# Three delta-rule preparations side by side, and attention's value products as three 16-bit products

## The chip, the cores and the metric

The kernel runs on one core of one Trainium2 chip. The metric is the device time of one execution in microseconds (us). The engines are TensorE (PE in the profile; its weight loads are PEld), VectorE (DVE), ScalarE (ACT), GpSimd (POOL) and SyncE (SP, which issues nearly all DMAs). Each engine works through its own instructions in the order in which they were put into its queue.

## The reference

Two layers of an encoder over 1024 tokens of width 1024, batch 1, float32. Each layer normalizes its input, projects it to 3448 columns, runs three groups of heads on them, multiplies by a SiLU gate, projects back and adds the residual. Cut to the two groups that the change touches:

```python
def gated_delta_chunked(q, k, v, g, beta):          # 6 heads of 64, two directions, 16 chunks of 64
    cum = jnp.cumsum(g, axis=-1)
    d_incl = jnp.exp(jnp.where(incl, cum[..., :, None] - cum[..., None, :], -jnp.inf))
    a_mat = beta[..., :, None] * jnp.einsum('nhcid,nhcjd->nhcij', k, k) * d_strict
    rhs = jnp.concatenate([beta[..., None] * v, (beta * gam)[..., None] * k], axis=-1)
    sol = lax.linalg.triangular_solve(a_mat, rhs, left_side=True, lower=True, unit_diagonal=True)
    ...
    def step(s, inp):                               # carries the 64x64 state from chunk to chunk
        u = u0_c - w_c @ s
        o = qg_c @ s + p_c @ u
        s = ge_c * s + kd_c.T @ u
        return s, o

def attend(q_blk):                                  # 6 heads, keys of 96 = 64 + 32 rotary, values of 64
    s = jnp.einsum('bqhd,bkhd->bhqk', q_blk, k)
    p = jax.nn.softmax(s, axis=-1)
    return jnp.einsum('bhqk,bkhd->bqhd', p, v)
```

The third group, RWKV-7, is scanned in chunks in the same way and is not changed.

## The kernel before

Each of the two layers (`layer`, L578) runs two streams of work at once. The **dense** stream (`dense_work`, L605) is a generator: the input projection (27 tiles of 128 columns, each as three 16-bit products, lines L371 to L373), then multi-head latent attention (`mla`, L1559). It yields, after each piece, a number of "units" that says how long the piece is held to be (0.65 for a group of three 512-column products). The **chain** stream is first the RWKV scan and then the delta rule (`gdn`, L1227). `chain` (L1155) runs in turns of a loop: in each turn it advances the scan `S` by one piece and each running preparation by one piece, and after each of these calls `tick`, which lets the dense stream advance by `dense / len(turn)` units. So the constant `DENSE_R` (RWKV) or `DENSE_G` (delta rule) is the number of dense units in one turn. What the turns record is then put in order on each engine by a scheduler; the TensorE orders of the two streams are tied to each other.

A **preparation** (`gdn_prep`, L1020) treats two chunks in both directions for two heads. It loads decays by DMA (`spread`, L1038), forms `gd_d`, `gd_pt`, `gd_g`, `gd_kb`, and then inverts a triangular matrix (`invert`, L897) in five doubling steps: a product into bank `pb` (L916), DVE's `z` (L942), its copy into a block-diagonal tile by ACT (L920) for one half and DVE (L921) for the other, then a product into `pb` and four into the bank `pe` (L959), evicted by ACT (L947, L960). There are 24 preparations per layer. `AHEAD_G = 2` lets two run at once, a new one starting when the last has made 10 pieces. Products into `pb` go to the bank of their parity (`B`, L304), of which 256 of 512 columns are used. A **step** of the scan (`gdn_step`, L1082) does one chunk: DVE makes `gs_r`, ACT `gs_u`, DVE the new state `gs_s`, with POOL's `gs_e` (L1104) as the decayed old state.

In **attention** the unit is a pair of heads and one half of the queries (`mla_main`, L1747): for each of 8 blocks of 128 keys and each head, three score products into one PSUM bank `pa` (L1765 to L1767), the exponential by ACT into a float32 tile `mp` (L1769), a running sum of these by POOL (L1771) for the denominator, and the product with the values in float32 (L1776). `pa` has three banks, one of which holds the unit's result. The rows' maxima come from products of their own (`mla_max`, L1732) that DVE reduces (L1733). `mla_v` (L1661) makes the values once per layer, in float32. `out_part` (L1855) does the part of the output projection that needs RWKV alone; it loads the residual by DMA into `mp` tiles and stores the sum.

## Time and profile before

| what | value |
|---|---|
| median of 3 runs | 2484.49 us (2482.22 to 2487.52) |
| the profiled execution | 2482.41 us, of which the span from the first to the last instruction is 2480.6 us |
| granted TensorE clock, mean | 0.952 |
| busy: PE, DVE, ACT, POOL | 91%, 66%, 56%, 35% of the span |
| layer 0, projection and RWKV | 0 to 585 us |
| layer 0, delta rule with attention | 585 to 1172 us |
| layer 0, output projection | 1172 to 1245 us |
| layer 1, the same three | 1245 to 1804, 1804 to 2395, 2395 to 2480.6 us |

The span is that of one profiled execution. A matmul's record is longer than the time it keeps PE from the next one, since matmuls are pipelined and their ends are modelled; the distance from one start to the next is what PE spends on it when nothing is late. In a row of groups, "x" is the count, then come the busy time and the mean of one in ns, and behind the bar the idle time before them with what ended it.

### The profile page before, as it was taken

How to read it: one execution, taken by the hardware profiler on the slowest of the kernel's cores; microseconds unless marked ns; L12 is line 12 of the kernel's file. 1: busy time of each engine (PE TensorE's matmuls, PEld its weight loads, DVE VectorE, ACT ScalarE, POOL GpSimd, SP SyncE). 2: the span in 40 equal slices, each digit the busy share in tenths (PEclk: the TensorE clock that was granted, in tenths of full speed). 3: DMA queues.
4: the chain of work that ended last, by engine and by line, in shares of the span. 5: the costliest groups of instructions: out<-in, count | busy, mean ns of one | idle time of the engine just before them, and what ended most of it. 6: DMA issues, size and time to landing. Idle time of an engine off the chain costs nothing.

```text
span 2480.6 us, 54956 instructions
## 1 busy us (share of the span) xinstructions
PE 2257.7 (91%) x21524; PEld 1384.0 (56%) x21524; DVE 1642.2 (66%) x3706; ACT 1384.2 (56%) x3077; POOL 865.8 (35%) x1095
## 2 busy tenths in 40 slices
PE   5999988999899999988989999899998999898988
PEld 4455655555576555554755565565556755555556
DVE  6557777755687766685345676877456777667755
ACT  5567556655555655555245765567464456455541
POOL 1133323323324544554012332342332256344430
PEclk9999999999899989999999999998998899899989
DMA  3121222213251111103212222222224311111041
GB/s 128 42 71 48 74 56 71 70 55 121 97 181 45 37 53 31 31 27 90 94 64 56 63 63 69 65 69 58 102 82 141 121 46 30 48 41 36 21 141 68
DMA packets 140338, 174.09 MB, mean 70 GB/s; under 512 B 37072, under 2 KB 95536, under 8 KB 140080
## 3 DMA queue, kind: packets, MB, share of 16 engines
q1 hardware_dynamic: 139936, 170.19, 22.8%
q8 instruction: 170, 2.79, 0.5%
q14 instruction: 88, 0.72, 0.1%
q0 software_dynamic: 144, 0.39, 0.1%
HBM read 106.88 MB, written 39.04 MB: 59 GB/s over the span
## 4 chain that ended last, share of the span: by engine, by line
PE 56%; DVE 20%; ACT 7%; issue 7%; POOL 5%; DMA 5%; SPq 0%; POOLq 0%; ACTq 0%; DVEq 0%
PE pa L371 5%; PE pa L372 5%; PE pa L373 5%; PE pa L1776 4%; PE pb L916 4%; DMA wf<-in_w_in_dram 3%; POOL wl L532 3%; PE pe L1339 2%; PE pa L1732 2%; DVE cacc L728 2%; PE pa L1765 2%; PE pe L833 2%; PE pe L959 2%; PE pc L1107 1%; PE pa L1767 1%
## 5 line engine op out<-in xcount | busy, mean ns | idle before, releaser
L373 PE MATMUL pa<-h,wl 128*128 128x512 f16 x864 | 332.4, 385 | 10.0 <-POOL wl L532 6.7
L371 PE MATMUL pa<-h,wh 128*128 128x512 f16 x864 | 333.7, 386 | 1.3 <-DVE h L484 1.3
L372 PE MATMUL pa<-h,wh 128*128 128x512 f16 x864 | 332.8, 385 | 0.0
L942 DVE TENSOR_TENSOR z<-pb,c 128x256 f16<-128x256 f32 (+1 forms) x320 | 155.3, 486 | 146.8 <-PE pb L916 141.1
L1771 POOL TENSOR_TENSOR md<-md,mp 128x512 f32<-128x512 f32 x144 | 192.2, 1337 | 149.5 <-ACT mp L1769 140.9
L920 ACT COPY bdz<-z 64x256 f16<-64x256 f16 (+1 forms) x384 | 173.4, 455 | 119.9 <-DVE z L942 95.1
L532 POOL TENSOR_TENSOR wl<-wf,wh 128x512 f16<-128x512 f32 x108 | 136.7, 1282 | 233.7 <-ACT wh L531 199.9
L947 ACT CAST x<-pb 128x256 f16<-128x256 f32 (+1 forms) x320 | 134.8, 421 | 106.1 <-PE pb L916 104.8
L960 ACT CAST xT<-pe 128x512 f16<-128x512 f32 x256 | 151.0, 590 | 55.6 <-PE pe L959 54.2
L1776 PE MATMUL pa<-mp,mv 128*64 128x512 f32 x384 | 177.0, 621 | 0.0
L1733 DVE TENSOR_REDUCE mmx<-pa 128x1 f32<-128x512 f32 x192 | 130.5, 685 | 34.4 <-PE pa L1732 32.0
L1404 POOL TENSOR_TENSOR rs_e<-rs_z,rw_em 64x128 f32<-64x128 f32 x120 | 55.7, 479 | 270.4 <-DVE rs_z L1431 242.0
L921 DVE COPY bdz<-z 64x256 f16<-64x256 f16 (+1 forms) x384 | 138.8, 365 | 13.1 <-PE pe L952 1.6
L1769 ACT ACTIVATE mp<-pa 128x512 f32<-128x512 f32 x192 | 114.6, 597 | 56.4 <-PE pa L1767 54.1
L916 PEld LDWEIGHTS <-bdgh 128*128 128x128 f16 x1920 | 92.1, 100 | 87.5 <-issue 52.8
L373 PEld LDWEIGHTS <-wl 128*128 128x128 f16 x864 | 85.5, 99 | 89.4 <-POOL wl L532 10.1
L916 PEld LDWEIGHTS <-xT 128*128 128x128 f16 x1600 | 77.3, 99 | 98.6 <-issue 64.9
L371 PEld LDWEIGHTS <-wh 128*128 128x128 f16 x864 | 90.0, 104 | 65.6 <-issue 10.8
L916 PE MATMUL pb<-z,xT 128*128 128x64 f16 x1600 | 108.6, 196 | 16.6 <-DVE z L942 15.6
L728 DVE SCALAR_TENSOR_TENSOR cacc<-raw,dv,cacc 128x512 f32<-128x512 f32 x144 | 120.8, 859 | 1.2 <-ACT cacc L722 0.7
L372 PEld LDWEIGHTS <-wh 128*128 128x128 f16 x864 | 85.5, 99 | 62.6 <-issue 8.2
L916 PE MATMUL pb<-x,bdgh 128*128 128x64 f16 x1600 | 106.1, 197 | 10.2 <-DVE x L937 7.2
(463 smaller groups left out, 5658.6 us busy)
## 6 DMA issues: line engine op xcount, KB each, us to landing
wf<-in_w_in_dram SPq DMA_DIRECT2D x54, 512.0 KB
q_d<-cacc SPq DMA_DIRECT2D x18, 512.0 KB
rw_ka<-rw_kr SPq DMA_DIRECT2D x32, 256.0 KB
rw_ka<-rw_ak SPq DMA_DIRECT2D x64, 128.0 KB
gate_d<-gate SPq DMA_DIRECT2D x16, 512.0 KB
wof<-in_w_out_dram SPq DMA_DIRECT2D x16, 512.0 KB
xp_d<-mp SPq DMA_DIRECT2D x32, 256.0 KB
xo<-xp_d SPq DMA_DIRECT2D x16, 512.0 KB
```

Of the source, the lines that this page charges most:

```text
L371: self.did = nc.tensor.matmul(out, lhsT=lh, rhs=rh, start=(first and idx == 0), stop=False)
L372: self.did = nc.tensor.matmul(out, lhsT=lh, rhs=rl, start=False, stop=False)
L373: self.did = nc.tensor.matmul(out, lhsT=ll, rhs=rh, start=False, stop=(last and idx == n - 1))
L532: nc.gpsimd.tensor_tensor(out=wl[:, ks], in0=wf[:, ks], in1=wh[:, ks], op=ALU.subtract)
L728: nc.vector.scalar_tensor_tensor(out=acc[:, c], in0=raw[:, c.start + k:c.stop + k], scalar=tap(k), in1=acc[:, c], op0=ALU.mult, op1=ALU.add)
L916: self.did = nc.tensor.matmul(ps[:, 64 * u:64 * u + 64], lhsT=st(lhsT, u), rhs=rhs(u), start=True, stop=True)
L920: nc.scalar.copy(zb[self.H[0], :, 0], t[self.H[0]])
L921: nc.vector.tensor_copy(zb[self.H[1], :, 1], t[self.H[1]])
L942: nc.vector.tensor_tensor(out=self.q8(z), in0=v(ps), in1=self.m8(self.c2(f"w{k}"), w), op=ALU.mult)
L960: nc.scalar.copy(xn[:, g:g + 4].rearrange("p u h i -> p (u h i)"), p2)
L1771: nc.gpsimd.tensor_tensor(out=acc[h], in0=prev[h] if t == 1 else acc[h], in1=pT, op=ALU.add)
L1776: self.did = nc.tensor.matmul(po[NR[h]], lhsT=vv[:, t, 2 * pr + h], rhs=pT[h], start=(t == 0), stop=(t == 7))
```

## The change

**Delta rule.** Three preparations run at once (`AHEAD_G` 3), a new one starting after 6 pieces of the last (the chain's argument 10 becomes 6). The block-diagonal tiles and the parities become three. The two banks `pb` are cut in halves of 256 columns, of which three are used (`halves`). `gd_g` no longer has a tile of its own but overwrites `gd_d`, behind `gd_pt`; `gs_r` and `gs_e` have one buffer instead of two; the result tile `X` is allocated at the end of the inversion. `DENSE_G` goes from 1.03 to 1.38 and `DENSE_R` from 1.0 to 0.95.

**Attention.** The values are scaled to the range of 16-bit floats (their scale is found with a reduction and a small product) and kept as a high and a low 16-bit part (ACT and DVE). The exponential is computed twice: in float32 and, as the high part, in 16 bits; the low part is their difference, by DVE for the first head and by POOL for the second. The product with the values is then high*high + low*high + high*low, with the two heads in turn. The first block's exponential is written straight into the running sum. The dense stream's number for the value products goes from 1.45 to 0.7 units. `mp` has 2 buffers instead of 5.

When the program is recorded it counts its turns and units. Before, a layer's RWKV scan takes 193 turns and its delta rule 279, with 246.3 of the 526.9 dense units done when RWKV ends. With the change it is 193 and 189 turns, and 236.55 of 490.9 units. In both the dense stream is exhausted when the delta rule ends.

```diff
-AHEAD_G = 2
+AHEAD_G = 3
...
-DENSE_R = 1.0
-DENSE_G = 1.03
+DENSE_R = 0.95
+DENSE_G = 1.38
...
     def B(self):
         if self.sx:
             return self.A()
+        if self.halves:
+            return self.halves[self.pty // 2][:, 256 * (self.pty % 2):256 * (self.pty % 2) + 256]
         return self.pb.tile([128, 512], F32, tag=f"b{self.pty}", name=self.nm("pb"))
...
+        self.ebias = self.cp.tile([128, 1], F32, name="ebias")
+        nc.vector.memset(self.ebias, math.log(16.0))
...
-        with self.phase("G", 6, "right"):
+        with self.phase("G", 5, "right"):
...
-        g = T("g", 1)
+        pt = T("pt", k)
+        nc.vector.tensor_tensor(out=fd(pt), in0=of(1), in1=fd(dd), op=ALU.mult)
+        g = dd
         nc.vector.tensor_tensor(out=fd(g), in0=of(0), in1=fd(dd), op=ALU.mult)
...
-        pt = T("pt", k)
-        nc.vector.tensor_tensor(out=fd(pt), in0=of(1), in1=fd(dd), op=ALU.mult)
...
-        X = T("x", k)
+        X = lambda: T("x", k - 1)
         yield
-        yield from self.invert(g, X)
+        X = yield from self.invert(g, X)
...
-            r = self.T("gs_r", [128, 2, 64], F32, 2)
+            r = self.T("gs_r", [128, 2, 64], F32, 1)
...
-                se = self.T("gs_e", [128, 2, 64], F32, 2)
+                se = self.T("gs_e", [128, 2, 64], F32, 1)
...
-                ps.append(thread(preparation, nxt, nxt % 2))
+                ps.append(thread(preparation, nxt, nxt % max(2, self.sets)))
...
     def gdn(self):
-        self.inv_tiles(2 * GW, 2)
-        self.chain([lambda hp=hp: self.gdn_open(hp) for hp in range(3)], 16 // GW, AHEAD_G, 0, 10, DENSE_G, self.gdn_prep, self.gdn_step, self.gdn_close)
+        self.inv_tiles(2 * GW, AHEAD_G)
+
+        self.halves = [self.pb.tile([128, 512], F32, tag=f"b{y}", name=self.nm("pb")) for y in range(2)]
+        self.chain([lambda hp=hp: self.gdn_open(hp) for hp in range(3)], 16 // GW, AHEAD_G, 0, 6, DENSE_G, self.gdn_prep, self.gdn_step, self.gdn_close)
+        self.halves = None
...
-        self.mv = self.T("mv", [128, 8, 6, 64], F32, 1)
+        c = self.U("mvs", [128, 5], F32, 2)
+        nc.vector.tensor_reduce(out=c[:, 0:1], in_=f, axis=AX.X, op=ALU.max, apply_absolute_value=True)
...
+        self.vs = c[:, 3:4]
+        self.mv = [self.T("mv" + x, [128, 8, 384], F16, 1) for x in "hl"]
...
-            nc.scalar.copy(self.mv[:, t].rearrange("p a v -> p (a v)"), ps[:, :384])
+            vh, vl = self.mv[0][:, t], self.mv[1][:, t]
+            nc.scalar.mul(vh, ps[:, :384], c[:, 4:5])
+            nc.vector.scalar_tensor_tensor(out=vl, in0=ps[:, :384], scalar=c[:, 4:5], in1=vh, op0=ALU.mult, op1=ALU.subtract)
...
-            pT = self.T("mp", [128, 512], F32, 5)
-            nc.scalar.activation(pT, ps, AF.Exp)
+            pT = self.T("mp", [128, 512], F32, 2) if t else acc[h]
+            nc.scalar.activation(pT, ps, AF.Exp, bias=self.ebias)
+            ph, pl = self.T("mph", [128, 512], F16, 4), self.T("mpl", [128, 512], F16, 4)
+            nc.scalar.activation(ph, ps, AF.Exp, bias=self.ebias)
+            (nc.vector, nc.gpsimd)[h].tensor_tensor(out=pl, in0=pT, in1=ph, op=ALU.subtract)
             if t:
-                nc.gpsimd.tensor_tensor(out=acc[h], in0=prev[h] if t == 1 else acc[h], in1=pT, op=ALU.add)
-            return pT
+                nc.gpsimd.tensor_tensor(out=acc[h], in0=acc[h], in1=pT, op=ALU.add)
+            return ph, pl
 
         def values(t, pT):
-            for h in range(2):
-                self.did = nc.tensor.matmul(po[NR[h]], lhsT=vv[:, t, 2 * pr + h], rhs=pT[h], start=(t == 0), stop=(t == 7))
+            for n, (a, b) in enumerate(((0, 0), (0, 1), (1, 0))):
+                for h in range(2):
+                    c = slice(128 * pr + 64 * h, 128 * pr + 64 * h + 64)
+                    self.did = nc.tensor.matmul(po[NR[h]], lhsT=vv[a][:, t, c], rhs=pT[h][b], start=(t == 0 and n == 0), stop=(t == 7 and n == 2))
...
-                yield 1.45
+                yield 0.7
                 values(t - 1, prev)
...
-        nc.scalar.copy(oT, po)
+        nc.scalar.mul(oT, po, self.vs)
...
-                xr = self.T("mp", [128, 512], F32, 5)
+                xr = self.T("mp", [128, 512], F32, 2)
```

Line numbers of the changed kernel differ from those before by some 6 to 27.

On **PE**, in layer 0's attention, the two value products of a block (`mv`, L1776, one for each head's `mp`) stood apart before, with products of `mla_max` (L1732) and of the inversion (L916) between them:

```order
L1732 MATMUL pa_14039<-mk_13042,mq_13543 128x512
L1776 MATMUL pa_13731<-mp_13877,mv_9172 64x512
L1732 MATMUL pa_14058<-mk_13042,mq_13543 128x512
L916 LDWEIGHTS bdgh_978_6606
L916 MATMUL pb_14061<-i_79,bdgh_978_6606 128x64
L916 LDWEIGHTS bdgh_978_6606
L916 MATMUL pb_14061<-i_79,bdgh_978_6606 128x64
L916 LDWEIGHTS bdgh_978_6606
L916 MATMUL pb_14061<-i_79,bdgh_978_6606 128x64
L916 LDWEIGHTS bdgh_978_6606
L916 MATMUL pb_14061<-i_79,bdgh_978_6606 128x64
L1776 MATMUL pa_13731<-mp_13939,mv_9172 64x512
```

Now the six of a block (L1803; `mph` and `mpl` are the high and low parts of the exponentials, `mvh` and `mvl` those of the values) mostly follow each other, the heads taking turns:

```order
L1803 LDWEIGHTS mvh_9612
L1803 MATMUL pa_12182<-mph_12300,mvh_9612 64x512
L1803 LDWEIGHTS mvh_9612
L1803 MATMUL pa_12182<-mph_12321,mvh_9612 64x512
L1803 LDWEIGHTS mvh_9612
L1803 MATMUL pa_12182<-mpl_12301,mvh_9612 64x512
L1803 LDWEIGHTS mvh_9612
L1803 MATMUL pa_12182<-mpl_12322,mvh_9612 64x512
L1803 LDWEIGHTS mvl_9613
L1803 MATMUL pa_12182<-mph_12300,mvl_9613 64x512
L1787 MATMUL pa_12429<-mq_10937,mk_11436 128x512
```

Over the whole program 136 of the 192 value products stood alone before, 24 times two were next to each other and twice four. Now the 576 products stand in 66 runs of one, 38 of two, 30 of three, 4 of four, 32 of five and 28 of six.

On **ACT**, in the same stage, two preparations' copies into their block-diagonal tiles (`bdz`, L920) followed each other before, and one exponential (L1769) stood for each score bank:

```order
L1769 ACTIVATE mp_11928<-pa_11924 128x512
L920 COPY bdz_977_6604<-z_2215_11940 64x4x64
L920 COPY bdz_980_6610<-z_2217_11949 64x4x64
L947 CAST x_2220_11964<-pb_11959 128x256
L960 CAST xT_2221_11966<-pe_11967 128x512
L1109 COPY gs_u_12004<-pc_11977 128x128
L1769 ACTIVATE mp_12010<-pa_12006 128x512
```

Now there are three preparations' copies (L926) and two exponentials from each bank (L1791, L1793), the second of them sometimes behind copies of the chain:

```order
L1791 ACTIVATE mp_12770<-pa_12766,ebias 128x512
L926 COPY bdz_972_6539<-z_2231_12754 64x4x64
L926 COPY bdz_975_6545<-z_2232_12762 64x4x64
L1793 ACTIVATE mph_12772<-pa_12766,ebias 128x512
L926 COPY bdz_969_6533<-z_2237_12781 64x4x64
L953 CAST x_2239_12792<-pb_6547 128x256
L960 CAST x_2241_12799<-pe_12794 128x256
L1791 ACTIVATE mp_12805<-pa_12801,ebias 128x512
L1793 ACTIVATE mph_12807<-pa_12801,ebias 128x512
```

On **POOL** each block of keys now brings, beside the two running sums (L1796, `md`), the second head's low part (L1794):

```order
L1796 TENSOR_TENSOR md_12184<-md_12184,mp_12562 128x512
L1794 TENSOR_TENSOR mpl_12565<-mp_12562,mph_12564 128x512
L1058 TENSOR_TENSOR gd_kg_12954<-gd_kg_12954,gd_qk_11691 128x256
L1796 TENSOR_TENSOR md_12183<-md_12183,mp_12649 128x512
L1796 TENSOR_TENSOR md_12184<-md_12184,mp_12687 128x512
L1794 TENSOR_TENSOR mpl_12690<-mp_12687,mph_12689 128x512
```

Before, only the sums stood there; the low part stands behind the sum of its own head.

More of the change, by code (lines that the diff above doesn't have):

```diff
@@ L1380, in rwkv_prep @@
         side = beside()
-        for _ in self.invert(g, XT):
+        for _ in self.invert(g, lambda: XT):
             next(side, None)
```

16 lines of the change are left out of this document (12 added, 4 removed).

## The prediction

> **What bounds the kernel now.** I read the page's first part, then one row for each stretch of the program, then the costliest groups of the delta-rule stretch, and then the order of time where these rows could mislead. The page says:
>
> ```profile
> span 2480.6 us, 54956 instructions
> PE 2257.7 (91%) x21524; PEld 1384.0 (56%) x21524; DVE 1642.2 (66%) x3706; ACT 1384.2 (56%) x3077; POOL 865.8 (35%) x1095
> ```
>
> PE looks full. The change lies in two stretches, the delta rule with attention in each layer, with a small shift out of the RWKV stretch before each. Busy time by stretch (length; PE, PEld, DVE, ACT, POOL; clock, DMA):
>
> ```profile
> 0.00:585.00 585.00, 517.84 (x5096) 312.82 (x5097) 385.62 (x876) 356.84 (x749) 173.16 (x226) 0.97 0.26 73
> 585.00:1172.00 587.00, 539.40 (x5337) 321.81 (x5337) 408.37 (x922) 324.43 (x769) 260.82 (x326) 0.95 0.22 67
> 1804.00:2395.00 591.00, 540.76 (x5338) 324.08 (x5337) 408.30 (x917) 324.04 (x768) 259.49 (x323) 0.94 0.22 66
> 880.00:980.00 100.00, 93.50 (x874) 52.32 (x873) 64.53 (x136) 47.12 (x111) 42.59 (x54) 0.90 0.15 46
> 780.00:880.00 100.00, 93.00 (x934) 51.96 (x934) 74.39 (x162) 61.45 (x148) 60.15 (x71) 1.00 0.13 39
> ```
>
> The two delta-rule stretches are alike, so I work one out and double it: 589 us on average, of which PE is busy in 540 (0.92) and DVE in 408 (0.69). Two things hold PE's 0.92 down as a measure. First, its records overlap. A 512-column 16-bit product has a record of 0.38 us but lets the next one start after 0.23:
>
> ```profile
> 301.91 0.39 PE L372 MATMUL pa<-h,wh 128*128 128x512 f16 x1
> 302.14 0.38 PE L373 MATMUL pa<-h,wl 128*128 128x512 f16 x1
> 302.36 0.40 PE L916 MATMUL pb<-x,bdz 128*128 128x64 f16 x8
> ```
>
> Second, short waits for DVE and ACT lie under the tails of those records. So PE has more slack than 49 us in a stretch. What paces it is the loop of the chain: 279 turns in 589 us is 2.11 us a turn, in which DVE has only 408 / 279 = 1.46 us of work and POOL 261 / 279 = 0.94. A turn is as long as the way of one preparation through PE, DVE and ACT and the dense work between.
>
> **The value products on PE.** One head's float32 product alone:
>
> ```profile
> 1007.02 1.07 PE L1776 MATMUL pa<-mp,mv 128*64 128x512 f32 x2
> 1008.02 0.50 PE L1765 MATMUL pa<-mq,mk 97*128 97x512 f32 x1
> 2241.80 1.08 PE L1776 MATMUL pa<-mp,mv 128*64 128x512 f32 x4
> 2242.82 0.23 PE L916 MATMUL pb<-x,bdgh 128*128 128x64 f16 x2
> ```
>
> It takes 1.00 us to the next start (two records each). Both heads next to each other (four records) take 1.02: they use two halves of PE's columns and run at once. Of the 192 products 136 stand alone in the order, 24 times two and twice four are together: 136 x 1.00 + 24 x 1.02 + 2 x 2.04 = 165 us, 82 a layer. The new products are 16-bit; each is a 512-column pass, 0.23 us. If neighbouring heads pair as the float32 ones do, the runs in the new order take 66 + 38 + 30 x 2 + 4 x 2 + 32 x 3 + 28 x 3 = 352 passes, 81 us or 40 a layer: **42 us less**. If they don't pair, 576 passes are 132 us, 66 a layer: 16 less. I take 36, near the pairing, since the row of four shows it.
>
> The Trainium skill (TensorEngine Tiling (Array Packing), Key Properties) says that changing the tiling mode drains TensorE, which speaks against many short runs. The row agrees in sign: 1.00 us for four passes of 0.23 leaves 0.08. By that rule the 198 runs that now stand for 162 would cost 36 x 0.08 = 3 us in all, so the sum is the same by either.
>
> **The moved projection work.** With 0.95 for 1.0 units a turn, 193 turns of RWKV take 9.75 units less and the delta rule's stretch that much more: 15 groups of three products, 45 x 0.22 = 10 us of PE. RWKV's stretch (PE 518 of 585) gives back between 0, if its turns are paced by the scan, and 10; I take 5 a layer.
>
> **What is added elsewhere, a layer.** The nearest groups, in the stretch 585 to 1172:
>
> ```profile
> L1769 ACT ACTIVATE mp<-pa 128x512 f32<-128x512 f32 x96 | 57.3, 597 | 28.2 <-PE pa L1767 27.0
> L1771 POOL TENSOR_TENSOR md<-md,mp 128x512 f32<-128x512 f32 x72 | 96.2, 1338 | 74.9 <-ACT mp L1769 70.6 <-PE pb L916 2.5 <-ACT gs_u L1109 0.6
> L1875 DVE TENSOR_TENSOR mp<-mp,pa 128x512 f32<-128x512 f32 x16 | 10.9, 683 | 2.7 <-PE pa L373 2.6
> L921 DVE COPY bdz<-z 64x256 f16<-64x256 f16 x144 | 51.3, 361 | 4.2
> L942 DVE TENSOR_TENSOR z<-pb,c 128x256 f16<-128x256 f32 x120 | 50.2, 419 | 37.5 <-PE pb L916 34.8 <-ACT gs_u L1109 1.8 <-ACT xT L960 0.3
> L973 DVE SCALAR_TENSOR_TENSOR z<-pb,cst 128x256 f16<-128x256 f32 x24 | 10.1, 420 | 8.2 <-PE pb L971 7.9
> ```
>
> - ACT: 96 more exponentials x 0.597 = 57 us, 324 to 381. In a stretch of 545 that is 0.70; off the path as a sum, but it holds a score bank 0.6 us longer, and of the three banks one is the unit's result.
> - POOL: 48 low parts. No row shows this form; by L1771 they are 48 x 1.34 = 64 us, 261 to 325.
> - DVE: 48 low parts of 512 columns x 0.683 (L1875) = 33 us, and 8 low parts of the values (384 columns, between L973's 0.42 and L1875's 0.68) = 4.
>
> DVE's 33 is a lower end, because **DVE and POOL get in each other's way**. Three operations of DVE, and then what POOL did in that time:
>
> ```profile
> 1076.06 1.31 DVE L921 COPY bdz<-z 64x256 f16<-64x256 f16 x1
> 1079.00 0.22 DVE L921 COPY bdz<-z 64x256 f16<-64x256 f16 x1
> 1077.61 0.71 DVE L932 TENSOR_TENSOR xT<-bdgh,wt 128x512 f16<-128x512 f16 x1
> 1076.01 1.28 POOL L1771 TENSOR_TENSOR md<-md,mp 128x512 f32<-128x512 f32 x1 [0.95 <-ACT mp L1769]
> 1077.37 0.67 POOL L911 TENSOR_TENSOR bdgl<-gd_g,bdgh 64x256 f16<-64x256 f32 x1
> ```
>
> The same copy takes 0.22 us where POOL is quiet and 1.31 where it began 0.05 behind a POOL addition, ending with it. L921's mean of 0.361 over 144 is 0.14 above that 0.22: 20 us. Another operation on SBUF alone:
>
> ```profile
> L1046 DVE TENSOR_TENSOR gd_d<-gd_d,c 128x256 f32<-128x256 f32 x23 | 13.3, 580 | 2.4 <-DMA gd_d<-dec_d 2.2
> ```
>
> Against the 0.419 of L942, which reads PSUM with as many columns, it loses 23 x 0.16 = 3.7 us. Seven such groups stand in a preparation, so I estimate the loss in the 408 at 20 + 7 x 3.7, some 46 to 50 us. With POOL busy 325 of 545 (0.60) for 261 of 587 (0.44) it grows by a third or more, 18 us.
>
> The 48 new DVE operations read two SBUF tiles and wait as well, by 0.15 each, 7 us. The Trainium skill (SBUF — State Buffer, Who interferes with whom) states the rule: a DVE instruction with two SBUF inputs, or a copy in a two-port mode, and a GpSimd instruction that reads SBUF exclude each other, and the later fully blocks. The trace agrees with its 0.22 and 1.31. DVE then has 408 + 33 + 4 + 18 + 7 = **470 us** a layer.
>
> **Turns.** 189 turns instead of 279 means that each has 470 / 189 = 2.49 us of DVE work and about 2.7 of PE records (540 - 36 + 10 = 514 over 189). A turn's latency of 2.11 is now below the work in it, so the three preparations cover each other's waits and the stretch is set by the fullest engines, DVE and PE. How full can DVE get? In the fullest window shown it was 0.74, while PE reached 0.92 as an average. I take 0.87, nearer to PE, because three preparations leave more that is ready: 470 / 0.87 = 540. From PE: its 514 plus the 49 idle of now gives 563, plus a third of that idle gives 530; 540 lies between.
>
> Two small things come on top. The first is in the loads of `out_part`; one of them in the chain of waits, and all 16 of layer 0:
>
> ```profile
> 691.74 3.83 DMA mp<-in_x_dram
> L1870 SPq DMA_DIRECT2D mp<-in_x_dram x16: 327/434/1315, 665.9 to 719.1; - x16
> ```
>
> `out_part` has two `mp` buffers for its residual, so a load waits for the store two tiles before, and on SP everything behind it waits too. One such load took 3.83 us here, and 16 tiles go by in 53 us (3.3 each); with load, addition (0.68) and a store of like length, two buffers allow one tile in 4.2, so 0 to 14 us a layer; I take 5, since dense work can fill in, which makes the stretch **545 us**. `gd_d` is held longer, until POOL's low part of the matrix, but the next preparation starts six pieces later and needs it only then: nothing, and some 2 us for each of 24 if that cover were gone (its DMA wait above is 2.2 in all).
>
> **Sum**, against the profiled execution's 2482.4: 2 x (545 - 589) = -88, RWKV 2 x -5 = -10, so 2384; the median stands 2 us above that execution, so **2386**. Ends: a stretch of 470 / 0.92 = 511 with RWKV's 10 gives 2308; one of 575 (PE 563 with `out_part`'s 12) and nothing from RWKV gives 2456.
>
> **The rivals.**
>
> *A, PE follows fully.* DVE isn't the limit, because much of its loss was waiting that overlaps; the stretch falls to about 500 (189 turns x 2.65). Time 2484 - 178 - 15 = 2291. For it: PE starts can be 0.23 apart under records of 0.38. Against: DVE at 0.94.
>
> *B, the low part is late.* The attention part alone, in the same columns as above:
>
> ```profile
> 780.00:1172.00 392.00, 360.65 (x3460) 201.66 (x3461) 273.95 (x589) 216.14 (x513) 200.70 (x234) 0.96 0.15 46
> ```
>
> The products of a block now need POOL's low part, which stands in POOL's queue behind two additions: 1.34 x 2 + 1.34 = 4.0 us of POOL for each block, beside the chain's. From 780 to 1172 POOL is busy 201 of 392 now and would be 265 of 350. Blocks are 392 / 48 = 8.2 us apart and would be 7; where they bunch, PE waits at `mpl`, with all dense and chain products behind it. One us for two thirds of 48 blocks is 32 a layer: stretch 577, time 2484 - 24 - 5 = 2455.
>
> *C, slower: DVE behind POOL.* Place: DVE's queue in the attention part. DVE has 470 us of work, and if the exclusion with POOL keeps its share at the 0.74 of its fullest window, the stretch is 470 / 0.74 = 635, time 2484 + 92 = 2576. It decides at a share of 0.80: there 470 / 0.80 = 588, the stretch of now. For it: no window shows DVE above 0.75, and in 780 to 1172 alone DVE's 274 becomes about 335 of what would be 350. Against: at 0.74 PE was still the busier one, so 0.74 isn't shown to be a ceiling.
>
> *D, the change does half of what it says*: the preparations stay paced by the single `pe` bank, which each holds from its products to ACT's eviction, and three reach it in the same turn (6 pieces apart, two turns to a doubling step). Turns then grow with the waits and the stretch stays near 589 less PE's 26: part of B's numbers, and with a little bad luck no change.
>
> **How the numbers follow.** My forecast 0.54, A 0.13, B with D 0.19, C 0.14. The range reaches from 2310 (into A's upper part) to 2465 (all of B but D's no change). About 0.2% is what a measurement of this kernel can tell from none, 5 us: no change gets 0.04, from D and the break-even of C; slower 0.12; faster 0.84.
>
> **What would show it.** Right: starts of neighbouring `mph`/`mpl` products in pairs under 0.03 us apart and the next 0.23 later, L1803 with some 80 to 90 us of starts in all; the delta-rule stretch 545 us with DVE near 0.87 of it; L921's mean above 0.4 us; RWKV's stretches 580 and 554. Wrong: idle time of PE before `mpl` products ended by POOL (B), DVE at 0.75 with PE waiting for `z` and the copies (C), PE waiting before `pe` products for ACT (D), or DVE idle a fifth of a stretch of 500 (A).

## The result and the profile after

The changed kernel takes **2619.47 us** (median of 4 runs, 2615.24 to 2626.03) against 2485.93 of the kernel before (4 runs on the same chip): a ratio of **1.0535, 95% interval 1.0517 to 1.0553**. The change costs 134 us; the forecast was a gain of about 100.

The page of the changed kernel, the same two lines that the prediction showed of before:

```profile
span 2616.2 us, 55789 instructions
PE 2277.8 (87%) x21720; PEld 1421.0 (54%) x21720; DVE 1781.8 (68%) x3829; ACT 1506.7 (58%) x3269; POOL 984.8 (38%) x1197
```

PE has fewer passes to make for the values, and yet its records add up to 20 us more than before. Busy time by stretch of the program (length; PE, PEld, DVE, ACT, POOL; clock, DMA); the rows are layer 0's RWKV and delta rule, the same two of layer 1, and two pieces out of layer 0's delta rule:

```profile
0.00:575.00 575.00, 511.30 (x5070) 307.80 (x5071) 396.00 (x869) 353.15 (x745) 170.31 (x229) 0.96 0.26 73
575.00:1241.00 666.00, 560.05 (x5456) 347.94 (x5456) 466.65 (x987) 389.01 (x870) 322.82 (x374) 0.87 0.20 60
1308.00:1855.00 547.00, 500.75 (x5004) 301.43 (x5004) 379.46 (x800) 335.84 (x703) 162.30 (x213) 0.98 0.24 67
1855.00:2532.00 677.00, 570.25 (x5561) 354.86 (x5558) 471.59 (x996) 392.31 (x876) 326.67 (x380) 0.87 0.20 60
1000.00:1100.00 100.00, 79.87 (x706) 46.56 (x702) 67.97 (x138) 59.18 (x129) 59.35 (x65) 0.81 0.11 28
1180.00:1241.00 61.00, 44.09 (x301) 21.52 (x302) 38.31 (x55) 32.53 (x59) 35.68 (x27) 0.81 0.26 83
```

All the loss is in the two delta-rule stretches: 666 and 677 us, where they were 587 and 591. RWKV's stretches are shorter, by 10 and 12. In the long stretches the work is almost what the prediction added up (DVE 467 for 470, ACT 389 for 381, POOL 323 for 325), but no engine is full: DVE's share is 467 / 666 = 0.70, not 0.87, and PE's granted clock has gone from 0.95 to 0.87. In the fifth row PE stands a fifth of the time, and no other engine is above 0.68.

What PE waits for in layer 0's stretch (engine, tile and line <- what it waited for: us in total, times, longest). After:

```profile
PE pa L1787 <- ACT mph L1793: 17.8, 10, 8.0
PE pa L1803 <- POOL mpl L1794: 14.9, 14, 2.6
```

and, for the kernel before, in its stretch 585 to 1172, PE's largest wait:

```profile
PE pb L916 <- DVE z L942: 5.4, 12, 1.0
```

L1787 is the score product, which waits until ACT has read an earlier score bank; L1803 are the value products. The same stretch in order of time shows how the two hang together. This is one stall in layer 0 of the changed kernel (start, us, engine, line, operation, in brackets the idle time before it; other operations that lie between are left out):

```profile
904.43 0.41 PE L1803 MATMUL pa<-mph,mvh 128*64 128x512 f16 x2
904.67 0.38 PE L1803 MATMUL pa<-mpl,mvh 128*64 128x512 f16 x1
904.81 1.26 POOL L1796 TENSOR_TENSOR md<-md,mp 128x512 f32<-128x512 f32 x1
904.84 1.78 DVE L1794 TENSOR_TENSOR mpl<-mp,mph 128x512 f16<-128x512 f32 x1
906.03 1.60 POOL L1794 TENSOR_TENSOR mpl<-mp,mph 128x512 f16<-128x512 f32 x1
907.66 0.69 ACT L1791 ACTIVATE mp<-pa,ebias 128x512 f32<-128x512 f32 x1 [2.57 <-POOL mpl L1794]
907.68 0.59 PE L1803 MATMUL pa<-mpl,mvh 128*64 128x512 f16 x1 [2.63 <-POOL mpl L1794]
907.68 1.01 PE L1803 MATMUL pa<-mph,mvl 128*64 128x512 f16 x2
```

DVE's low part of the first head starts 0.03 us behind POOL's addition and takes 1.78 us. POOL's low part of the second head starts beside it and takes 1.60. PE has done three of the block's six products and stands 2.63 us for the fourth, with everything of the chain behind it; ACT stands 2.57, since the next exponential needs an `mp` buffer that POOL is reading. Each engine does what comes next in its own queue, and two of them have their next instruction behind POOL's.

How long these operations take over the stretch (line, engine, operation, tiles, count, then busy time and mean ns, then the idle time before them):

```profile
L1794 DVE TENSOR_TENSOR mpl<-mp,mph 128x512 f16<-128x512 f32 x42 | 45.6, 1086 | 2.8 <-ACT mph L1793 2.4
L1794 POOL TENSOR_TENSOR mpl<-mp,mph 128x512 f16<-128x512 f32 x42 | 53.4, 1272 | 0.1
L1791 ACT ACTIVATE mp<-pa,ebias 128x512 f32<-128x512 f32 x84 | 57.8, 688 | 48.8 <-PE pa L1789 30.3 <-POOL mpl L1794 12.0 <-DVE mpl L1794 4.5
L1793 ACT ACTIVATE mph<-pa,ebias 128x512 f16<-128x512 f32 x96 | 65.3, 683 | 0.1
L1787 PE MATMUL pa<-mq,mk 128*128 128x512 f32 x48 | 26.4, 551 | 6.8 <-ACT mph L1793 5.6 <-DVE mmx L1755 1.3
L927 DVE COPY bdz<-z 64x256 f16<-64x256 f16 x144 | 53.5, 380 | 5.2 <-PE pb L977 1.0
```

and the score product as it was before:

```profile
L1765 PE MATMUL pa<-mq,mk 128*128 128x512 f32 x48 | 23.8, 496 | 1.8 <-ACT mp L1769 1.5
```

The same score product takes 0.551 us for 0.496, 1.11 times as long; the clocks of the two stretches, 0.95 and 0.87, differ by 1.09. It also fits PE's account: the prediction expected 514 us of PE records in this stretch; at a clock of 0.87 for 0.95 that is 514 x 0.95 / 0.87 = 561, and 560 were measured. So close an agreement is in part luck, since the 514 takes a saving counted in starts from a sum of records.

The pairing of the two heads came out where a block's products stand together. Three rows of PE in order of time:

```profile
829.01 0.41 PE L1803 MATMUL pa<-mph,mvh 128*64 128x512 f16 x2
829.25 0.38 PE L1803 MATMUL pa<-mpl,mvh 128*64 128x512 f16 x2
829.47 0.38 PE L1803 MATMUL pa<-mph,mvl 128*64 128x512 f16 x2
```

Two products end within 0.41 us, where each alone has a record of 0.4, and the next two start 0.24 and 0.22 us later: six products in the time of three. Over the whole program 206 pairs of value products start within 0.03 us of each other, near the 224 (576 - 352) of the prediction's count. Yet the value products' time on PE, each counted to the next start or to its own end where PE then stands, is 127 us, where the same count gives 167 for the float32 ones before: 20 us a layer less, not 36.

### The profile page after: what moved, and what is told of

Same layout as the page of the kernel before. It is cut to its first block, busy times and chain, and to the rows that moved or that the text cites. A ratio compares the mean times of both kernels' runs of the same rounds, so it can differ in the third digit from the quotient of the medians.

```text
span 2616.2 us, 55789 instructions
## 1 busy us (share of the span) xinstructions
PE 2277.8 (87%) x21720; PEld 1421.0 (54%) x21720; DVE 1781.8 (68%) x3829; ACT 1506.7 (58%) x3269; POOL 984.8 (38%) x1197
## 5 line engine op out<-in xcount | busy, mean ns | idle before, releaser
L926 ACT COPY bdz<-z 64x256 f16<-64x256 f16 (+1 forms) x384 | 172.3, 456 | 164.4 <-DVE z L948 136.9
L1796 POOL TENSOR_TENSOR md<-md,mp 128x512 f32<-128x512 f32 x168 | 224.8, 1340 | 98.8 <-ACT mp L1791 85.2
L1791 ACT ACTIVATE mp<-pa,ebias 128x512 f32<-128x512 f32 x168 | 115.7, 689 | 97.7 <-PE pa L1789 62.0
L927 DVE COPY bdz<-z 64x256 f16<-64x256 f16 (+1 forms) x384 | 145.6, 386 | 14.3 <-PE pb L977 2.0
L1787 PE MATMUL pa<-mq,mk 97*128 97x512 f32 x192 | 108.6, 566 | 46.9 <-ACT mph L1793 33.1
L1793 ACT ACTIVATE mph<-pa,ebias 128x512 f16<-128x512 f32 x192 | 130.8, 683 | 0.2
L965 PE MATMUL pe<-xT,bdz 128*128 128x128 f16 x1024 | 111.2, 235 | 20.6 <-DVE bdz L927 9.7
L374 PEld LDWEIGHTS <-wh 128*128 128x128 f16 x864 | 90.4, 105 | 67.2 <-issue 8.9
L965 PEld LDWEIGHTS <-bdz 128*128 128x128 f16 x1280 | 87.6, 104 | 66.7 <-issue 19.6
```

The lines of the kernel that those rows point to most:

```text
L374: self.did = nc.tensor.matmul(out, lhsT=lh, rhs=rh, start=(first and idx == 0), stop=False)
L926: nc.scalar.copy(zb[self.H[0], :, 0], t[self.H[0]])
L927: nc.vector.tensor_copy(zb[self.H[1], :, 1], t[self.H[1]])
L965: self.did = nc.tensor.matmul(p2[:, 128 * u:128 * u + 128], lhsT=st(zb, g + u), rhs=st(xT, g + u), start=True, stop=True)
L1796: nc.gpsimd.tensor_tensor(out=acc[h], in0=acc[h], in1=pT, op=ALU.add)
```

## The experiments

The change has three parts that can be separated: the dense work moved out of RWKV's stretch (`DENSE_R` 0.95), the delta-rule part, and attention's values. At first two theories stood against each other: **P**, that the attention part's own chain of score bank, two exponentials and POOL's low part stalls PE, and **F**, that the three preparations' fuller turns crowd DVE and ACT. All ratios are to the kernel before, run on the same chip; the interval is 95%. Where two runs are subtracted below, their medians are, as us; a few us of that are uncertain, since they come from several chips, on which the kernel before took 2482.8 to 2487.5 us.

### The parts alone

The delta-rule part (with the moved work), attention as before; lines without a sign tell in words what the edit keeps:

```diff
 AHEAD_G = 3, halves, single gs_r and gs_e, gd_g in gd_d: as in the change
-DENSE_G = 1.38
+DENSE_G = 1.58
 mla_v, mla_main, mla_tail, out_part: as before
```

> The changed kernel with its attention part undone: float32 values, one exponential, five mp buffers; three preparations stay, and the units of a turn are 1.58 so that the larger dense work ends with the 189 turns. Theory P (the attention part's new chain, score bank to ACT to POOL's low part, is what stalls): the delta-rule stretches are 550 to 590 us, the time 2400 to 2490. Theory F (three preparations in fuller turns crowd DVE and ACT, whatever attention does): the stretches stay above 630, the time above 2560.

Measured: 2467.43 us, 0.9924 (0.9898 to 0.9950). One execution of the same kernel on another chip took 2474.40:

> A look for comparison only: the three preparations with attention as before, a second time, on this chip. 2460 to 2475 us by every theory.

The values (with the moved work), the delta-rule part as before:

```diff
 mla_v, mla_main, mla_tail, out_part: as in the change
-AHEAD_G = 3
-DENSE_G = 1.38
+AHEAD_G = 2
+DENSE_G = 0.935
 gdn_prep, gdn_step, gdn, invert, chain: as before
```

> The changed kernel with its delta-rule part undone: two preparations, 279 turns of 0.935 units; the 16-bit value products stay. Theory P: PE still waits for the low parts (some 15 us of a stretch) and for banks that the second exponential holds (some 40), and the time is above 2560. Theory F: with turns as light as before, PE's 36 us a layer come through, time 2420 to 2480.

Measured: 2564.19 us, 1.0314 (1.0272 to 1.0355). So the values cost without a third preparation, and the delta-rule part gains: F alone is wrong. But 0.9924 x 1.0314 is 1.0236, and the whole change is at 1.0535: something of 70 us and more comes only when both are there. Both of these kernels, and all that are built on the changed one, also keep two small edits of the change: five scratch buffers for six in the delta rule's phase (`phase("G", 5)`) and a `dynamic_dma_scratch_size` of 2048 for 8192, which the shortened difference further up doesn't show. No run prices these two by themselves.

### What in the values costs: order, buffers, or the work itself

Four runs keep the arithmetic and change the order or the buffers. In the whole change, the high part copied from the float32 exponential, so that the score bank is free one exponential earlier:

```diff
-            nc.scalar.activation(ph, ps, AF.Exp, bias=self.ebias)
+            nc.scalar.copy(ph, pT)
```

> The changed kernel with the high part of the exponential copied by ACT from the float32 tile instead of computed a second time from the score bank, which is free after the first exponential. Theory P: PE's idle time before score products ended by the second exponential (40 us of a stretch) falls below 15, the time to 2540 to 2590. Theory F: no change, 2610 to 2630, as ACT's work is the same.

Measured: 2613.80 us, 1.0509 (1.0481 to 1.0537), the whole change's time. PE's wait for ACT before the score product (L1787) falls from 33.1 to 24.1 us over the program, and its wait for POOL's low part rises from 27.6 to 40.2: the wait has moved. Both low parts on DVE:

```diff
-            (nc.vector, nc.gpsimd)[h].tensor_tensor(out=pl, in0=pT, in1=ph, op=ALU.subtract)
+            nc.vector.tensor_tensor(out=pl, in0=pT, in1=ph, op=ALU.subtract)
```

> The changed kernel with the low parts of both heads on DVE, none on POOL. Theory P: PE's 15 us of idle time before POOL's low parts and ACT's 12 behind them go, 2560 to 2600. Theory F: DVE gets 45 us a layer more and the time rises to 2640 or more.

Measured: 2584.08 us, 1.0388 (1.0350 to 1.0425): 35 us less although DVE, the fuller of the two engines, has all of it. Its low part then takes less on average than before:

```profile
L1794 DVE TENSOR_TENSOR mpl<-mp,mph 128x512 f16<-128x512 f32 x168 | 160.1, 956 | 3.3 <-ACT mph L1793 2.0
L1791 ACT ACTIVATE mp<-pa,ebias 128x512 f32<-128x512 f32 x168 | 115.8, 689 | 83.1 <-PE pa L1789 60.4 <-POOL md L1796 7.9 <-DVE mpl L1794 7.0
```

In layer 0's attention, from its first score to its last, DVE is now fuller than in any row shown of the kernel before:

```profile
807.00:1213.00 406.00, 341.98 (x3282) 205.59 (x3281) 321.64 (x597) 255.71 (x552) 201.84 (x221) 0.89 0.13 38
```

That is 322 of 406 us, 0.79. So DVE's amount of work isn't the limit. What POOL no longer does is part of the price: its load itself, or the passing of the block between DVE and POOL; this run doesn't separate the two. On the values alone, five `mp` buffers as in the kernel before:

```diff
-            pT = self.T("mp", [128, 512], F32, 2) if t else acc[h]
+            pT = self.T("mp", [128, 512], F32, 5) if t else acc[h]
```

> The values-alone kernel (two preparations) with five mp buffers for the float32 exponentials and residuals instead of two. If the two buffers are the cause (ACT waits for a buffer, holds the score bank and the chain's copies), its time falls from 2564 to 2500 or less. If the low parts' way through POOL and DVE is the cause, it falls by less than 25, to 2540 or more.

Measured: 2565.54 us, 1.0338 (1.0297 to 1.0380). And the value products one block later, with six buffers each for the parts:

```diff
-            if prev:
+            late.append(cur)
+            if t > 1:
...
-                values(t - 1, prev)
-            prev = cur
+                values(t - 2, late[t - 2])
```

> The values-alone kernel with the value products of a block issued one block later, and six buffers for the high and low parts so that they can wait. If PE's stop before late low parts is the cause (some 40 us of a stretch before the value products), the time falls from 2564 to 2480 to 2510. If buffers or ACT's work are the cause, it stays above 2540.

Measured: 2566.13 us, 1.0342 (1.0308 to 1.0376). Neither changed the time. With the products one block later PE's wait for POOL's low part falls from 16.5 to 5.1 us, and its wait for ACT before the score product rises from 19.2 to 28.2: the wait comes back elsewhere, and P as a story of one late tile is wrong too. What was left was the work itself. Two runs leave it out, and with it the waits for it. First, the subtractions: the low part isn't computed, and the high part is used in its place, so that PE has the same products:

```diff
-            (nc.vector, nc.gpsimd)[h].tensor_tensor(out=pl, in0=pT, in1=ph, op=ALU.subtract)
...
-            return ph, pl
+            return ph, ph
```

> The values-alone kernel without the subtractions: the low part of the exponentials is left out and the high part takes its place in the product, so PE and ACT have the same work. If the low parts (their lateness and their hold on DVE and POOL) are the cause, the time falls to 2440 to 2490. If the second exponential on ACT is the cause, it stays above 2530.

Measured: 2508.99 us, 1.0113 (1.0079 to 1.0146). Then also the float32 exponential, but for a unit's first block; POOL sums the 16-bit one:

```diff
-            nc.scalar.activation(pT, ps, AF.Exp, bias=self.ebias)
+            if not t:
+                nc.scalar.activation(pT, ps, AF.Exp, bias=self.ebias)
...
-                nc.gpsimd.tensor_tensor(out=acc[h], in0=acc[h], in1=pT, op=ALU.add)
+                nc.gpsimd.tensor_tensor(out=acc[h], in0=acc[h], in1=ph, op=ALU.add)
```

> As the kernel without subtractions, and also without the float32 exponential (but for a unit's first block): the 16-bit one alone is computed, and summed by POOL. PE's work is the same. The difference from the kernel without subtractions is the price of the second exponential and the mp buffers: under 15 us by the theory of the late low parts, 50 or more if ACT is the cause. With both gone PE's saving should come through: 2420 to 2460.

Measured: 2461.59 us, 0.9923 (0.9892 to 0.9953). The low parts cost 55 us and the second exponential 47, on engines that are never full. The attention part of layer 0, from its first score to its last, in these three kernels (columns as above). The values alone:

```profile
787.00:1196.00 409.00, 351.83 (x3252) 207.10 (x3251) 302.48 (x565) 260.30 (x567) 252.94 (x269) 0.90 0.13 37
```

without the low parts:

```profile
796.00:1172.00 376.00, 336.75 (x3254) 200.17 (x3254) 248.68 (x518) 259.12 (x568) 189.83 (x223) 0.93 0.14 40
```

and with one exponential:

```profile
786.00:1147.00 361.00, 324.61 (x3266) 196.00 (x3265) 241.43 (x518) 215.72 (x486) 179.23 (x223) 0.92 0.15 42
```

54 us less on DVE and 63 less on POOL (their times beside each other, not after one another) shorten it by 33; 43 less on ACT (with 7 and 11 on DVE and POOL) by another 15. DVE stands at 302 / 409 = 0.74 in the first row and at 0.66 and 0.67 in the others. The same passes of PE (3252 to 3266 records) go from 352 us of records to 325.

### Where the two parts collide

If the collision were this added load meeting three preparations, then without the load the three should pay again. The whole change, with both omissions of the last two runs:

> The change as it is, without its two subtractions and without the float32 exponential but for a unit's first block (as in the two runs on the values alone; the low part is left out and the high part used in its place, so the output is less exact). PE has all of the change's products. This asks what the interaction of the two parts hangs on. Load theory: the added work on ACT, DVE and POOL is what the three preparations collide with; without it their gain of about 20 us comes on top of the 21 us of the values' products, so 2425 to 2455 us. Order theory: three preparations and a shorter attention on PE collide by themselves, whatever the elementwise work: 2480 to 2530 us.

Measured: 2490.48 us, 1.0011 (0.9994 to 1.0029). That is 129 us below the whole change, but 29 above the same attention with the delta-rule part as before: the delta-rule part doesn't pay, although the added load is gone. The load theory of the collision is wrong for the most of it.

The next candidate was the units: with 0.7 a block for 1.45, blocks might come closer together. The whole change with the old count:

```diff
-DENSE_G = 1.38
+DENSE_G = 1.58
...
-                yield 0.7
+                yield 1.45
```

> The whole change, but a block's value products are counted as 1.45 units of dense work as before (and 1.58 units a turn), not 0.7. This asks whether the smaller count bunches attention's blocks so that their exponentials and low parts pile up. If it does, the wait for the low part falls and the time goes to 2540 to 2590 us; if the load on the three engines is the cause whatever the spacing, it stays within 2600 to 2635 us.

Measured: 2603.90 us, 1.0478 (1.0448 to 1.0507): about 15 us less, between the two expectations and nearer to no effect. The next run tells what the moved work by itself does, in the kernel before:

```diff
-DENSE_R = 1.0
-DENSE_G = 1.03
+DENSE_R = 0.95
+DENSE_G = 1.065
```

> The kernel before with 0.95 for 1.0 units of dense work a turn in RWKV's stretch, and 1.065 for 1.03 in the delta rule's so that the moved units are done in the same turns; nothing else. If the 20 us that the three preparations alone gained come from this move, 2460 to 2472 us; if they come from the third preparation, 2480 to 2492 us.

Measured: 2505.30 us, 1.0071 (1.0046 to 1.0095): it costs. RWKV ends 10 us earlier, but the delta rule's stretch, from its start to attention's first score and from there to the last, now is

```profile
566.00:777.00 211.00, 185.82 (x1956) 125.21 (x1953) 142.20 (x358) 111.46 (x263) 62.33 (x95) 0.91 0.36 114
777.00:1181.00 404.00, 373.40 (x3425) 208.33 (x3426) 264.73 (x553) 213.44 (x508) 197.98 (x233) 0.93 0.14 39
```

where before it was

```profile
576.00:770.00 194.00, 178.12 (x1943) 120.10 (x1941) 129.98 (x330) 105.36 (x251) 57.47 (x91) 0.92 0.37 117
770.00:1162.00 392.00, 364.43 (x3485) 204.40 (x3487) 273.83 (x577) 218.23 (x519) 202.89 (x239) 0.96 0.14 42
```

17 and 12 us longer, for 10 us of products. More of the same move costs on top of the three preparations too:

```diff
-DENSE_R = 0.95
-DENSE_G = 1.58
+DENSE_R = 0.90
+DENSE_G = 1.63
```

> The three preparations with attention as before, and 0.90 for 0.95 units of dense work a turn in RWKV's stretch (1.63 for 1.58 in the delta rule's). If RWKV's stretch gives back about 10 us a layer for each such step and the delta rule's takes less than that, 2445 to 2460 us; if the delta rule's stretch now takes as much as RWKV's gives, 2463 to 2480 us.

Measured: 2497.44 us, 1.0045 (1.0022 to 1.0068), 30 us above the same with 0.95, and outside both expectations. With the move priced, the values alone cost 2564 - 2505 = 59 us, and the delta-rule part without the move gains 2505 - 2467 = 38. Together they would be 2526 us, so 93 of the whole change's 2619 come only when both are there. Without the added work the same difference is 2490 - 2462 + 38 = 67: two thirds of the collision stay when the work is left out. Does the third preparation collide? The whole change with two at once:

```diff
-AHEAD_G = 3
-DENSE_G = 1.38
+AHEAD_G = 2
+DENSE_G = 1.10
```

> The whole change, but with two preparations at once for three (and 1.10 units of dense work a turn for 1.38, in 238 turns for 189, so that the work is done in the same stretch). If the third preparation is what collides with the values' longer elementwise work, about the time of the values alone: 2550 to 2585 us. If the collision is in the rest (the matrix in gd_d's place, single buffers of gs_r and gs_e, the halves of the pe bank), 2605 us or more.

Measured: 2651.74 us, 1.0665 (1.0631 to 1.0698). And the delta-rule part alone with two at once (`AHEAD_G` 2, `DENSE_G` 1.255 in the first experiment's kernel):

> The three preparations alone (attention as before), but with two at once for three, 1.255 units a turn in 238 turns. If the third preparation brings the gain, 2480 us or more; if the move of the projection work does, 2460 to 2475 us as with three.

Measured: 2517.75 us, 1.0124 (1.0093 to 1.0155). So the third preparation pays in both: 50 us with attention as before, 32 in the whole change. The collision is there with two as well: on the changed delta-rule part the values cost 2652 - 2518 = 134 us (152 with three), on the old one 59. Two of the remaining edits were tried. Fuller turns, put into the values alone (the second preparation 6 pieces behind the first, not 10, with 1.10 units a turn):

```diff
-...16 // GW, AHEAD_G, 0, 10, DENSE_G, ...
+...16 // GW, AHEAD_G, 0, 6, DENSE_G, ...
```

> The values alone, with the delta-rule part of before but for the start of the second preparation, 6 pieces behind the first and not 10: 238 turns for 279, 1.10 units of dense work a turn for 0.935. If fuller turns are what the values' elementwise work collides with, it goes from 2564 towards the whole change with two preparations, 2610 to 2655 us. If it is the other edits, 2550 to 2580 us.

Measured: 2570.46 us, 1.0361 (1.0322 to 1.0401): not that. And the whole change with two buffers for `gs_r` and `gs_e`, and three for `mpl` to make room:

```diff
-            r = self.T("gs_r", [128, 2, 64], F32, 1)
+            r = self.T("gs_r", [128, 2, 64], F32, 2)
...
-                se = self.T("gs_e", [128, 2, 64], F32, 1)
+                se = self.T("gs_e", [128, 2, 64], F32, 2)
```

> The whole change with two buffers for gs_r and gs_e, as before, and three for mpl to make the room. If the scan's single buffers tie it to the late queues, 2560 to 2600 us; if they have no part in it, 2605 to 2635 us.

Measured: 2623.59 us, 1.0553 (1.0505 to 1.0602): no gain from that either, though the `mpl` buffer that had to go could hide one.

**What stays open** is thus which of the delta-rule part's other edits collides with the values: the halves of two banks for whole banks, the matrix in `gd_d`'s place, the late allocation of `X`, or their sum. The trace has one trait that goes with these edits. DVE's first instruction on `gd_d` waits for the decays' DMA, in the kernel before and in the changed one over both layers:

```profile
DVE gd_d L1046 <- DMA gd_d<-dec_d: 3.4, 5, 0.9
DVE gd_d L1054 <- DMA gd_d<-dec_d: 44.5, 28, 5.3
```

While it waits, DVE's queue stands, with attention's low parts in it. But the delta-rule part alone, which gains, shows much of the same wait,

```profile
DVE gd_d L1054 <- DMA gd_d<-dec_d: 37.0, 26, 3.6
```

and the whole change with two preparations, slower than both, shows less of it (32.2 us, 21 times). So this isn't shown to be the cause; no run has a second `gd_d` buffer.

### A version without added work

The pairing can be had without 16-bit products: put the two heads' float32 products next to each other. On the three preparations, with attention as before, by a block that the scheduler keeps together:

```diff
-            for h in range(2):
-                self.did = nc.tensor.matmul(po[NR[h]], lhsT=vv[:, t, 2 * pr + h], rhs=pT[h], start=(t == 0), stop=(t == 7))
+            with self.tc.tile_critical():
+                for h in range(2):
+                    m = nc.tensor.matmul(po[NR[h]], lhsT=vv[:, t, 2 * pr + h], rhs=pT[h], start=(t == 0), stop=(t == 7))
```

> The three preparations, attention's float32 products as before, but each block's two products of the two heads stand next to each other in PE's order, behind a point that waits for the work issued so far on every engine. No work is added to ACT, DVE and POOL. 136 products that stood alone become 68 pairs, 68 x 0.98 = 67 us less of PE. If PE's saved work counts when nothing is added elsewhere, and the 96 points cost little, 2405 to 2445 us; if each point costs about 1 us, that eats it: 2460 to 2560 us.

Measured: 2688.05 us, 1.0806 (1.0755 to 1.0857). Each of the 96 points at which all engines meet costs (2688 - 2467) / 96 = 2.3 us if the pairing saved nothing, and (2688 - 2467 + 67) / 96 = 3.0 if it saved its 67. No run pairs them without such a point. The fastest kernel here that computes the whole result is the delta-rule part alone, with attention as before: 2467 us, under the 2486 of the kernel before.

## Why the prediction was wrong

**The sum, piece by piece.** In us, from the differences above, beside what the prediction gave the piece over both layers. Its sum went by DVE's work at a share of 0.87, so the predicted pieces are worked out from that share: 408 us of DVE now, 33 + 18 + 7 with the low parts, 4 with the values' scaling; this column adds up to the forecast's -98.

| piece | predicted | measured | from |
|---|---|---|---|
| projection work moved | -10 for RWKV; its 20 of products on PE not in the sum | +20 | 2505.3 - 2485.3 |
| delta-rule part, values as before | -240: 2 x (408 / 0.87 - 589) | -38 | 2467.4 - 2505.3 |
| values' products in 16 bits, with the values' scaling, the smaller unit count and POOL's sums on 16-bit tiles | +9: 2 x 4 / 0.87; -72 on PE not in the sum | -44 | 2461.6 - 2505.3 |
| second exponential | 0, "off the path as a sum" | +47 | 2509.0 - 2461.6 |
| low parts | +133: 2 x 58 / 0.87 | +55 | 2564.2 - 2509.0 |
| loads of `out_part` with two `mp` buffers | +10 | none seen | 2564.2 against 2565.5 with five |
| both parts together | not thought of | +93 | what is left to 2619.5 |

**The step that failed** is the one on turns: "the three preparations cover each other's waits and the stretch is set by the fullest engines". From it came DVE's share of 0.87, and with it the sign: the rise from 0.69 was to bring 240 us. The amounts of work were right to about 3% on DVE, ACT and POOL; the share of DVE in the whole change was 0.70. The first experiment shows the step by itself, three preparations with attention as before. Its delta rule of layer 0, ahead of attention and in it:

```profile
564.00:773.00 209.00, 185.65 (x2007) 123.89 (x2006) 145.06 (x360) 113.97 (x275) 65.27 (x103) 0.93 0.34 110
773.00:1154.00 381.00, 357.06 (x3398) 204.61 (x3398) 250.99 (x553) 209.69 (x498) 192.33 (x224) 0.95 0.14 41
```

These are 590 us with 396 of DVE, a share of 0.67; at 0.87 they would be 455. In the kernel before the same two stretches are 586 us with 404 of DVE, 0.69. PE isn't covered better either: it stands 47 us for 43. So with 189 turns for 279 each turn became longer in the same proportion. What holds the stretch there isn't shown; PE's records fill 0.92 of it, as before. The third preparation brought 50 us, by the run with two in its place; the part's other edits took 12 of them back (2518 - 2505), and the move of the projection work 20.

A second step failed beside it: ACT's second exponential was called off the path because ACT isn't full, and it cost 47 us. The low parts, which the sum did charge, cost less than it said. How such work costs time on engines that are never full is argued from the order of the queues and not shown as a sum: each block of attention goes through PE, ACT, DVE, POOL and PE again, and an added instruction can stand ahead of a copy that the chain's next product needs. The stall in the timeline above is 2.63 us of the 420 / 48 = 8.8 that a block has, with DVE, ACT and POOL at 0.70, 0.58 and 0.48 of the stretch. The largest piece, the 93 us of both parts together, has no shown cause.

**Then the clock.** PE's stops aren't only lost themselves. The granted clock in layer 0's attention was 0.96 before, 0.90 with the values alone and 0.87 in the whole change. The stall shown above has such a drop behind it. Rows of 3 us, in the columns of the stretches, and two score products out of them:

```profile
904.00:907.00 3.00, 1.05 (x19) 0.50 (x17) 2.56 (x4) 1.09 (x3) 2.85 (x4) 1.00 0.15 59
907.00:910.00 3.00, 2.32 (x24) 1.30 (x23) 0.00 (x0) 2.21 (x6) 3.00 (x4) 0.60 0.02 5
910.00:913.00 3.00, 3.00 (x12) 1.51 (x11) 0.29 (x1) 0.30 (x2) 2.18 (x3) 0.50 0.15 44
916.00:919.00 3.00, 2.74 (x26) 1.71 (x27) 2.67 (x5) 2.91 (x7) 2.07 (x2) 1.00 0.15 44
910.00 0.79 PE L1787 MATMUL pa<-mq,mk 97*128 97x512 f32 x1
916.00 0.50 PE L1787 MATMUL pa<-mq,mk 128*128 128x512 f32 x1 [0.18 <-ACT mph L1793]
```

PE stands from 905.05 to 907.68, then has work again, but at half the clock for some 7 us. This is the rule in this trace: in the 3.4 us ahead of a drop PE is idle for 0.52 of the time on average, against 0.12 of the time overall. Over the whole program the clock withheld is (1 - 0.915) x 2616 = 222 us, against (1 - 0.952) x 2481 = 119 before, 103 us more. The prediction kept the clock of before in every price of PE. The Trainium skill (TensorE: Matmul & The Clock Gate, A second HAM failure mode: psum-queue depth-cycling) tells of another kernel in which frequent micro-idles of PE between groups of products make the clock go up and down; the traces agree in direction, 0.87 where waits are many. How much of the 134 us is the clock and how much the waits isn't separated by these runs, since each brings the other.

**Other points of the prediction.**

- Pairing: right in the order, 206 pairs. "80 to 90 us of starts in all" was wrong: 127 us, in part at the lower clock.
- RWKV gives back 5 a layer: 10 and 12 were measured, the upper end. But the work that went over cost 29 us where it went in layer 0 of the run that did only this (17 + 12), and 11 in layer 1, against the 10 a layer that PE's products were priced at. The stretch had little room for it: the part ahead of attention was at 178 of 194 us of PE.
- The second exponential: 0.597 us, from a row without an operand for the bias, was too little: 0.688 and 0.683 were measured, 9 us more in a layer for each of the two that now stand there. The Trainium skill (ScalarE: Activation LUTs, What ACT_TABLE_LOAD costs) gives about 93 ns for each per-partition operand; the trace agrees with its 0.688 - 0.597 = 0.091. It was there to be read and was missed. ACT's sum, 389 for 381, shows about half of these 17.
- DVE's low part: 0.683 + 0.15 was taken, 1.086 was measured; between 0.68 and 1.79, with 1.78 in the stall above, where a POOL addition had begun 0.03 us earlier.
- `gd_d` "nothing, and some 2 us for each of 24 if that cover were gone": it was gone for 28 of the 48 preparations of both layers, 44.5 us, 1.6 each.
- `L921` (now L927) above 0.4 us: 0.380; the sign of exclusion there was smaller than expected, and it fell on the low parts.
- DENSE_G's effect: that a smaller number of units a turn sends more turns into the part ahead of attention wasn't considered. That part of layer 0 went from 194 us to 236 in the whole change and 231 with the values alone, and holds 2210 and 2344 products for 1943:

```profile
570.00:806.00 236.00, 206.78 (x2210) 138.57 (x2205) 163.35 (x422) 130.33 (x314) 68.45 (x105) 0.90 0.32 103
806.00:1226.00 420.00, 349.47 (x3285) 210.21 (x3284) 297.06 (x552) 256.65 (x554) 250.42 (x267) 0.87 0.13 37
```

```profile
556.00:787.00 231.00, 208.21 (x2344) 139.62 (x2343) 159.73 (x411) 127.64 (x301) 69.45 (x107) 0.92 0.33 110
```

  The first two rows are the whole change (ahead of attention, and attention), the third is the values alone. With the smaller number, part of attention's share of the chain is done earlier, so what attention gains and what the part ahead of it loses have to be read together.

**The rivals.** B's sign is there (PE before `mpl` ended by POOL, 14.9 us in layer 0) and so is C's (DVE at 0.70, below its break-even of 0.80). C, at 2576, was nearest in number, and right in that DVE's share doesn't rise; but 0.74 isn't a ceiling, as DVE reached 0.79 of attention when it was given POOL's half of the low parts as well. D, the single `pe` bank, isn't among PE's largest waits. A, PE followed by all, didn't come. The chance of 0.12 for slower was too small: no row stood behind a share of 0.87, B and C were priced as alternatives although the signs of both are there at once, and the clock, which neither counted, came on top.

## What to carry to other kernels

More work in flight doesn't by itself make an engine fuller: here a third preparation left DVE's share at 0.67, and a forecast that divides the work by a hoped-for share carries that hope whole into its sum. Nor is an engine at 60% of a stretch free: where several in-order engines hand one block around, added instructions cost a good part of their time even though none of these engines is near full (here 102 us for some 340 us of added records: 58 of exponentials, 51 and 61 of low parts on DVE and POOL in a layer). Before trading TensorE passes for elementwise work, look at what each added instruction stands ahead of in its queue, and price TensorE at the clock that its stops will leave it. Try each part of a combined change alone: here one part gains 20 us, or 38 without the shift of work that came with it, and the whole loses 134.

## What the runs showed of the hardware

- An exponential of 128x512 from PSUM takes 0.688 us with the bias as a tile's column and 0.597 with none.
- Two 16-bit products of 512 columns into the two halves of PE's columns run at once, 0.24 us for a pair.
- A point in the program at which all engines wait for each other cost 2.3 to 3.0 us, by the one run that had 96 of them.
- After PE stood for 2.63 us its clock was at half for some 7 us, and a score product took 0.79 us for 0.50.
- One DVE subtraction of two SBUF tiles of 128x512 takes 0.68 us or up to 1.79, and POOL's 1.14 up to 2.14, in one and the same kernel. Rows over layer 0's stretch of the changed kernel (min/median/max in ns; first and last start):

```profile
L1794 DVE TENSOR_TENSOR mpl<-mp,mph x42: 676/948/1787, 819.0 to 1233.2; 128x512 f16<-128x512 f32 x42
L1794 POOL TENSOR_TENSOR mpl<-mp,mph x42: 1143/1158/2135, 822.1 to 1236.4; 128x512 f16<-128x512 f32 x42
```
